# Second feed-forward layer in four parts of 6, 6, 4 and 6 blocks

## The chip, the cores and the metric

The kernel runs on one core of a Trainium2 chip. The metric is the device time of one execution in microseconds (us): 1334.24 us before the change, the median of three runs (1333.27 to 1334.41). TensorE is called PE here, VectorE DVE, ScalarE ACT, GpSimd POOL; SP is the engine that issues the DMAs.

## The reference

One encoder layer on x of shape (1, 1024 tokens, 1024 features), all in float32: two branches (chunked attention and a gated MLP over chunks) and their merge, then a SwiGLU feed-forward network and a final norm. The change touches the last three lines.

```
h = h + merged @ w_out
hn = rmsnorm(h, norm_ffn)
g, up = split(hn @ w_ffn_in)                # 2 x 2816 columns
h = h + (silu(g) * up) @ w_ffn_out          # 2816 -> 1024, the second layer
return rmsnorm(h, norm_final)               # x * rsqrt(mean(x*x) + 1e-6) * gain
```

## The kernel before

Features lie on the 128 partitions and tokens along the free axis; `h` is eight tiles (rows j = 0 to 7) of 128 x 1024. A float32 product is made from three PE passes over operands that are split into a high and a low part (`hi`, `lo`, type fp32r): hi x hi, hi x lo, lo x hi. ACT casts the high part, DVE or POOL subtracts it from the source for the low part.

Both feed-forward layers use a seven-product form (Strassen-Winograd): a 2x2 block product from seven products of sums instead of eight. `moving` names the right operands (b11, t1, t2, b21, t3, b22, t4), and products are called "1" to "7". Each leaves its result in one of three banks of PSUM (`bank_of`): "1" and "2" in c1, "5" and then "3" in c3, "6", "7", "4" in c2. A bank that is written on by the next of its products must first have been added by DVE to `h` or `first_g` (`collect_g`, L1509); that add is called an eviction here.

First layer (the loop at L1439): 22 blocks f of 128 inner features, seven products each of 12 matmuls of 128x512. Its products' evictions, activations and weight sums run on DVE, ACT and POOL beside PE. From product 32 on (L1450) the same loop also makes the weights of the second layer: `weights_g` (L1421) is a generator that for a part c and a row pair r loads two rows of `w_ffn_out`, forms four sums on DVE, casts seven high parts on ACT, subtracts seven low parts on DVE (`products_of`, L1220) and writes them by DMA to `g_dram`. One such group is ten steps; `take(making, 1 + (i % 8 == 0))` takes nine steps every eight products.

Second layer: 18 of the 22 blocks in three parts of six, in the seven-product form. A part has 4 r x 7 = 28 products of nine matmuls of 128x512 (`product_g`, L1502). While part c runs, `operands_g(c + 1)` (L1464) makes the right operands of the next: 21 steps, one per product, with a sum on DVE in 12 of them, a cast on ACT in all, and a low part in all, on DVE or POOL by the table LOW_G (9 and 12 in parts after the first). `prepare_g` (L1492) loads each product's weights from `g_dram` six products ahead. The last four blocks are multiplied plainly (`fo`, `split_act`, and the loop at L1607): for tokens 0 to 511, 512 to 767 and 768 to 1023 in turn, eight rows j of 12 matmuls, each followed by the eviction, ACT's square and scale of the row, and DVE's sum of squares `acc`. `finish(i)` (L1579) reduces the squares on PE (ss), takes the inverse root (a power on POOL), spreads it by PE (bc), and multiplies and stores the rows; it is woven into the next span of tokens.

Order on every engine is that of the code: instructions of one engine run in the order in which the loops issue them.

Of the kernel before, what the change touches and what calls it, by code (L numbers as in the profile page):

```python
# [11 lines left out]
F32 = mybir.dt.float32  # L12
# [4 lines left out]
P = 128  # L17
# [12 lines left out]
PARTS = 3  # L30
LAST = FB - 6 * PARTS
# [17 lines left out]
def encoder_block(ctx: ExitStack, tc: tile.TileContext, xT, w_in, w_v, w_vs, w_att, w_sgu, w_out,  # L49
# [1367 lines left out]
    order_g += [(c, r, p) for c in range(PARTS) for r in range(4) for p in ("1652734" if c else "65734")]  # L1417
    W3 = 3 * P
    g_dram = dram.tile([len(order_g), P, 2 * W3], F32, name="g_dram")

    def weights_g():  # L1421

        for c in range(PARTS):
            for r in range(4):
                rows = [slot(f"fo{c}_{j}") for j in (2 * r, 2 * r + 1)]
                for t, j in zip(rows, (2 * r, 2 * r + 1)):
                    nc.sync.dma_start(t[:, :2 * W3], w_ffn_out[j][:, c * 2 * W3:(c + 1) * 2 * W3])

                def sums():
                    t = slot(f"gs{c}_{r}", (P, 2, HALF))  # L1430
                    return t[:, 0, :W3], t[:, 1, :W3]

                yield from products_of(f"gw{c}_{r}", rows, W3,
                                       lambda p, t: nc.sync.dma_start(g_dram[order_g.index((c, r, p))], t), sums)
# [4 lines left out]
    for i in range(last_pair - 5):  # L1439
# [10 lines left out]
        if i >= MAKE_FROM:  # L1450
            take(making, 1 + (i % 8 == 0))
# [6 lines left out]
    staged, right_g, act = {}, {}, {}  # L1458
# [5 lines left out]
    def operands_g(c):  # L1464

        low = []
        one, two = ([staged.pop(6 * c + 3 * i + k) for k in range(3)] for i in range(2))
        x = {n: [t[:, halves[h]] for t in ts] for n, ts, h in
             (("b11", one, 0), ("b12", one, 1), ("b21", two, 0), ("b22", two, 1))}
        x.update(t1=x["b11"], t2=x["b11"], t3=x["b12"], t4=x["b21"])  # L1470
        sums = dict(t1=("b12", "b11"), t2=("b22", "t1"), t3=("b22", "b12"), t4=("b21", "t2"))
        n = 0
        for name in ("b11", "t1", "t2", "b21", "t3", "b22", "t4") if c else ("b11", "b21", "t1", "t2", "t3", "b22", "t4"):
            right_g[c, name] = []
            for k in range(3):
                src = x[name][k]
                if name in sums:
                    y, z = (x[m][k] for m in sums[name])
# [192 lines left out]
```

## Time and profile before

| what | value |
| --- | --- |
| median of the three timed runs | 1334.24 us |
| profiled execution, its span | 1334.2 us, 1332.5 us |
| PE busy, share of the span | 1308.0 us, 98% |
| DVE busy | 932.4 us, 70% |
| ACT busy | 571.6 us, 43% |
| POOL busy | 422.6 us, 32% |
| mean granted clock of PE | 0.996 of full speed |
| last chain, PE's share | 58% |

The span runs from the first to the last instruction of the profiled execution. Busy shares are averages over the whole program. The chain is followed back from the last instruction to what released each. Matmuls overlap in PE's pipeline, so the mean length of one (about 390 ns) is not what it costs; that is read from a long stretch without a gap, divided by its count.

### The profile page before, as it was taken

The page shows a single profiled execution, that of the slowest core. Times are in us where ns is not written, and L with a number is a line of the kernel's source. Part 1 is how long each engine was busy: PE and PEld are TensorE (multiplying, and loading weights), DVE is VectorE, ACT ScalarE, POOL GpSimd, SP SyncE. Part 2 cuts the span into 40 slices and gives each one's busy share as a digit, 9 for nine tenths or more (in the row PEclk, how much of TensorE's full clock was granted, in tenths as well). Part 3 has the DMA queues.
Part 4 walks back from the last instruction along what each step waited for, and adds up shares of the span by engine and source line. Part 5 has one row for each costly group of instructions (what it writes and reads, how often), then busy time and mean ns, then how long its engine had stood idle before and what let it go on. Part 6 is the DMA issues. An engine that isn't in the chain of part 4 may idle for free.

```text
span 1332.5 us, 17516 instructions
## 1 busy us (share of the span) xinstructions
PE 1308.0 (98%) x6290; PEld 1085.4 (81%) x6290; DVE 932.4 (70%) x1510; ACT 571.6 (43%) x1056; POOL 422.6 (32%) x343
## 2 busy tenths in 40 slices
PE   9999999999999999999999999999999999999997
PEld 7888888878887877888887888887888887888887
DVE  6257877871869778677867487878878857757445
ACT  7345666663434534454443034444444433212144
POOL 2525444324457345530000021221222222424242
PEclk9999999999999999999999999999999999999999
DMA  6001101003041221259873566666667658786723
GB/s 253 28 17 40 29 28 36 26 25 95 17 166 32 63 64 56 64 199 339 325 296 133 193 232 216 228 229 228 217 223 241 232 191 324 265 286 211 239 57 127
DMA packets 77879, 208.79 MB, mean 157 GB/s; under 512 B 8544, under 2 KB 12128, under 8 KB 77792
## 3 DMA queue, kind: packets, MB, share of 16 engines
q1 hardware_dynamic: 77792, 207.67, 45.3%
q8 instruction: 50, 0.82, 0.3%
q14 instruction: 37, 0.30, 0.1%
HBM read 140.01 MB, written 67.63 MB: 156 GB/s over the span
## 4 chain that ended last, share of the span: by engine, by line
PE 58%; DVE 3%; DMA 1%; issue 1%; ACT 0%; POOL 0%; DVEq 0%; ACTq 0%; POOLq 0%
PE c L182 41%; PE wo L1207 7%; PE mc L182 5%; PE last L168 3%; PE mp L182 2%; DMA g<-g_dram 1%; DVE gw L1227 0%; DVE s L1148 0%; DVE mergedlo L781 0%; DVE t3l L173 0%; DVE exact L1411 0%; DVE gs L1239 0%; DVE u L1360 0%; PE bc L276 0%; ACT wm_hi L155 0%
## 5 line engine op out<-in xcount | busy, mean ns | idle before, releaser
L1183 POOL TENSOR_TENSOR w_lo<-s,w_hi 128x512 fp32r<-128x512 f32 x54 | 77.8, 1443 | 324.4 <-ACT w_hi L1177 324.4
L182 PE MATMUL c<-t,g 128*128 128x512 f32 x432 | 103.7, 390 | 0.0
L182 PEld LDWEIGHTS c<-t,g 128*128 128x128 f32 x432 | 80.7, 188 | 18.3 <-DMA g<-g_dram 1.1
L1518 DVE TENSOR_TENSOR h_all<-h_all,c 128x512 f32<-128x512 f32 x72 | 49.0, 686 | 53.6 <-PE c L182 52.6
L1177 ACT CAST w_hi<-s 128x512 fp32r<-128x512 f32 x72 | 44.7, 621 | 93.9 <-DVE s L1148 93.7
L182 PE MATMUL c<-b,g 128*128 128x512 f32 x324 | 78.4, 389 | 0.4 <-DMA g<-g_dram 0.4
L182 PEld LDWEIGHTS c<-b,g 128*128 128x128 f32 x324 | 60.7, 188 | 13.4 <-issue 0.8
L504 ACT ACTIVATE p<-p,low 128x640 f32<-128x640 f32 (+4 forms) x64 | 44.6, 697 | 58.6 <-DVE low L496 58.4
L1482 ACT CAST t<-stage 128x512 fp32r<-128x512 f32 x36 | 22.2, 623 | 73.5 <-DVE stage L1479 68.1
L156 POOL TENSOR_TENSOR wm_lo<-wg,wm_hi 128x512 fp32r<-128x512 f32 x21 | 30.1, 1437 | 64.0 <-ACT wm_hi L155 60.2
L1207 PE MATMUL wo<-mergedhi,wo_hi 128*128 128x512 f32 x128 | 50.0, 391 | 0.0
L1207 PE MATMUL wo<-mergedhi,wo_lo 128*128 128x512 f32 x128 | 49.8, 389 | 0.0
L1207 PE MATMUL wo<-mergedlo,wo_hi 128*128 128x512 f32 x128 | 49.8, 389 | 0.0
L496 DVE CUSTOM_DVE_ANT_0 p<-s,bias 128x640 f32<-128x640 f32 (+4 forms) x64 | 41.7, 651 | 10.9 <-PE s L492 8.9
L260 POOL TENSOR_TENSOR rms_y<-rms_a,minus_half 128x4 f32<-128x4 f32 (+2 forms) x6 | 6.1, 1014 | 135.3 <-DVE rms_a L255 135.3
L1246 ACT CAST gw<-fo 128x384 fp32r<-128x384 f32 x60 | 30.4, 509 | 43.1 <-DMA fo<-in_w_ffn_out 19.2
L173 POOL TENSOR_TENSOR t<-stage,t 128x512 fp32r<-128x512 f32 x18 | 26.8, 1492 | 61.2 <-ACT t L1482 56.9
L522 DVE TENSOR_TENSOR ptl<-t,pth 128x640 fp32r<-128x640 f32 (+4 forms) x64 | 41.7, 651 | 4.5 <-ACT pth L521 4.2
L168 PE MATMUL last<-act_hi,fo 128*128 128x256 f32 (+1 forms) x192 | 43.8, 320 | 0.0
L1227 DVE TENSOR_TENSOR gw<-fo,gw 128x384 fp32r<-128x384 f32 x60 | 42.2, 703 | 0.9 <-ACT gw L1246 0.8
L506 DVE TENSOR_SCALAR p<-p,inv 128x640 f32<-128x640 f32 (+4 forms) x64 | 39.6, 619 | 2.2
L1357 ACT ACTIVATE g<-g 128x512 f32<-128x512 f32 x22 | 13.9, 633 | 62.8 <-DVE g L1356 62.8
(428 smaller groups left out, 4236.9 us busy)
## 6 DMA issues: line engine op xcount, KB each, us to landing
g_dram<-gw SPq DMA_DIRECT2D x84, 384.0 KB, 2.6
g<-g_dram SPq DMA_DIRECT2D x84, 384.0 KB, 3.7
f_dram<-fw SPq DMA_DIRECT2D x28, 512.0 KB, 4.1
act_dram<-u SPq DMA_DIRECT2D x44, 256.0 KB, 2.3
stage<-act_dram SPq DMA_DIRECT2D x22, 512.0 KB, 6.5
fg<-in_w_ffn_in SPq DMA_DIRECT2D x18, 512.0 KB, 5.0
fu<-in_w_ffn_in SPq DMA_DIRECT2D x18, 512.0 KB, 4.4
fo<-in_w_ffn_out SPq DMA_DIRECT2D x24, 384.0 KB, 4.5
```

The costliest lines, as they stand in the source:

```text
L168: nc.tensor.matmul(ps, w, x[:, s], start=k == 0 and i == 0, stop=k == kc - 1 and i == 2)
L182: nc.tensor.matmul(ps, w[:, ws], x, start=first and k == 0 and n == 0, stop=k == last and n == 2, skip_group_check=True)
L496: nc.vector.tensor_tensor_reduce(out=p[:, :w].rearrange("p (a c) -> p a c", a=parts), in0=ps[:, :parts, :c], in1=bias.rearrange("p (a c) - ...
L504: nc.scalar.activation(e["p"], e["p"], AF.Exp, bias=e["low"], scale=-1.0, accum_out=e["tot"])
L506: nc.vector.tensor_scalar(e["p"], e["p"], e["inv"], None, op0=OP.mult)
L522: nc.vector.tensor_tensor(out=lo[:, :w], in0=ps[:, :w], in1=hi[:, :w].bitcast(F32), op=OP.subtract)
L1177: nc.scalar.copy(hi, src)
L1183: nc.gpsimd.tensor_tensor(out=lo, in0=src, in1=hi.bitcast(F32), op=OP.subtract)
L1207: nc.tensor.matmul(banks_w[j, half], w, x, start=k == 0 and n == 0, stop=k == KB - 1 and n == 2, skip_group_check=True)
L1227: nc.vector.tensor_tensor(out=t[:, width:2 * width], in0=src, in1=t[:, :width].bitcast(F32), op=OP.subtract)
L1246: nc.scalar.copy(t[:, :width], src)
L1518: nc.vector.tensor_tensor(out=dst, in0=dst, in1=banks_g[name, r], op=OP.add)
```

## The change

The 22 blocks are taken in four parts of 6, 6, 4 and 6 (`SIZES`), all in the seven-product form; the plain blocks, their weights and their operands go. A product of the part of four has six matmuls instead of nine, and its weights are 128x256 instead of 128x384. `weights_g` has 16 groups instead of 12 and is advanced by three steps every two products. Operands of the last part are made from the fourth product of the part of four on (`OPERANDS_AT`). The last part follows its own order (`LAST_G`): its first 20 products finish the first 512 tokens and all of the other products but "5" and "3", which are done last, for tokens 512 to 767 and then 768 to 1023. Squares, scale and `finish` follow there row by row; the sum of squares of the first of these spans moves to POOL. The last eight weights lie in the general pool of slots.

```diff
-PARTS = 3
-LAST = FB - 6 * PARTS
+SIZES = (6, 6, 4, 6)
+BASES = (0, 6, 12, 16)
+PARTS = len(SIZES)
-H_AT, STAGE_AT = (0, 3, 5, 7), (8, 9, 11, 12, 13, 14)
+H_AT, OPERANDS_AT = (0, 3, 5, 7), (14, 12, 3)
+STAGE_AT = (8, 9, 11, 12, 13, 14, 33, 34, 35, 36, 51, 53, 55, 58, 60, 62)
+LAST_G = "10 11 12 20 13 21 60 22 61 23 70 62 71 40 63 41 72 73 42 43 50 51 30 52 31 53 32 33"
...
-    order_g += [(c, r, p) for c in range(PARTS) for r in range(4) for p in ("1652734" if c else "65734")]
+    order_g += [(c, r, p) for c in range(PARTS - 1) for r in range(4) for p in ("1652734" if c else "65734")]
+    order_g += [(PARTS - 1, int(x[1]), x[0]) for x in LAST_G.split()]
+    widths = [n // 2 * P for n in SIZES]
...
-            take(making, 1 + (i % 8 == 0))
+            take(making, 1 + (i % 2 == 0))
...
-    fo = [block(f"fo{j}", w_ffn_out[j][:, PARTS * 6 * P:], LAST * P, keep=hi_lo_slot,
-                lo_engine=nc.vector if j == 1 else None) for j in range(KB)]
...
-            t = wpool.tile([P, D], F32R, name=f"g{i}", tag=("raw", "raw", "hi", "lo", "hi", "lo")[i % 6])
-            nc.sync.dma_start(t[:, :2 * W3].bitcast(F32), g_dram[i])
+            w = widths[order_g[i][0]]
+            if i < len(order_g) - 8:
+                t = wpool.tile([P, D], F32R, name=f"g{i}", tag=("raw", "raw", "hi", "lo", "hi", "lo")[i % 6])
+            else:
+                t = slot(f"g{i}", dt=F32R)
+            nc.sync.dma_start(t[:, :2 * w].bitcast(F32), g_dram[i][:, :2 * w])
...
-        if p == "4" and c == PARTS - 1:
+        if c < PARTS - 1:
+            return
+        if p == "1":
             for row, half in ((0, 1), (1, 1), (1, 0)):
                 dst = h[2 * r + row][:, halves[half]]
                 nc.gpsimd.tensor_tensor(out=dst, in0=dst, in1=first_g[:, r], op=OP.add)
+        elif half == 0:
+            square_row(2 * r + row, 0)
+    def square_row(j, i):
+        s = slice(*token_parts[i])
+        x = h[j][:, s]
+        if n_squares[i] > 1:
+            (nc.gpsimd if i == 1 else nc.vector).tensor_tensor(out=acc[:, s], in0=acc[:, s], in1=squares[i], op=OP.add)
+        squares[i] = tmp(f"sq3_{i}_{j}")[:, :x.shape[1]] if n_squares[i] else acc[:, s]
+        nc.scalar.activation(squares[i], x, AF.Square)
+        nc.scalar.activation(x, x, AF.Copy, scale=g_fin[:, j:j + 1])
+        n_squares[i] += 1
...
-        prepare_g(i + 6)
+        if i == len(order_g) - 8:
+            break
+        prepare_g(i + 6 + 8 * (i > len(order_g) - 20))
...
+        if c < len(OPERANDS_AT) and n == OPERANDS_AT[c]:
+            coming = operands_g(c + 1)
...
+    end = finish(0)
+    for i, (a, b) in enumerate(token_parts[1:], 1):
+        cols = slice(a - HALF, b - HALF)
+        for n, m in enumerate(range(len(order_g) - 8, len(order_g))):
+            c, r, p = order_g[m]
+            if p == "5":
+                banks_g["c3", r] = dense_ps(f"c3_{i}_{r}")
+            ps = banks_g["c3", r][:, :b - a]
+            multiply(ps, parts_g[m], [[x[:, cols] for x in k] for k in right_g[c, moving[p]]], p == "5")
+            j = 2 * r + (p == "5")
+            dst = h[j][:, a:b]
+            nc.vector.tensor_tensor(out=dst, in0=dst, in1=ps, op=OP.add)
+            square_row(j, i)
+            take(end, {1: 1, 3: 2, 4: 1, 5: 1, 6: 1}.get(n, 0))
         drain(end)
         end = finish(i)
```

Three places show how instructions move. The first is DVE in the first layer's loop while the second layer's weights are made; before, `gs`, `fo` and `gw` are the sums, the loaded rows and the low parts of that work, the other names belong to the first layer.

```order
L1243 TENSOR_TENSOR fo_2_7249<-fo_2_7249 128x384
L1227 TENSOR_TENSOR gw_1_6_7389<-fo_2_7249,gw_1_6_7389 128x384
L1148 TENSOR_TENSOR s_7_7418<-fu_7209 128x512
L173 TENSOR_TENSOR w_lo<-fg_7207,w_hi 128x512
L1227 TENSOR_TENSOR gw_1_3_7414<-fo_2_7249,gw_1_3_7414 128x384
L1227 TENSOR_TENSOR gw_1_4_7438<-fo_3_7250,gw_1_4_7438 128x384
L1148 TENSOR_TENSOR s_7_7446<-s_7_7418,fg_7207 128x512
L1365 TENSOR_TENSOR u_6_7462<-c_6_7348,sg_7273 128x512
L1366 TENSOR_TENSOR u_6_7462<-u_6_7462,sg_7273 128x512
```

The same work after the change (line numbers are two or three higher):

```order
L1242 TENSOR_TENSOR gs_1_7253<-fo_3_7210 128x384
L1230 TENSOR_TENSOR gw_1_2_7283<-fo_2_7209,gw_1_2_7283 128x384
L1244 TENSOR_TENSOR fo_2_7209<-gs_1_7253,fo_2_7209 128x384
L1230 TENSOR_TENSOR gw_1_5_7308<-gs_1_7253,gw_1_5_7308 128x384
L1151 TENSOR_TENSOR s_6_7319<-fg_7081,s_6_7287 128x512
L1246 TENSOR_TENSOR fo_2_7209<-fo_2_7209 128x384
L1230 TENSOR_TENSOR gw_1_6_7313<-fo_2_7209,gw_1_6_7313 128x384
L1151 TENSOR_TENSOR s_6_7341<-fg_7081,fu_7083 128x512
L1354 TENSOR_TENSOR p_6_7357<-c_6_7344,sg_7281 128x512
```

Of nine instructions six instead of four belong to the weights of the second layer.

The second place is DVE while operands of a next part are made: before, those of the third part during the second, whose products have nine matmuls. `c_1_2` is a bank of part 1, r = 2 (counted from 0); rows at L1518 are evictions, L1479 sums, L173 low parts.

```order
L1518 TENSOR_TENSOR h_all<-h_all,c_1_2_10602 128x512
L1479 TENSOR_TENSOR stage_10468<-stage_10512,stage_10468 128x512
L173 TENSOR_TENSOR t_2_2_10647<-stage_10497,t_2_2_10647 128x512
L1518 TENSOR_TENSOR h_all<-h_all,c_1_2_10619 128x512
L1479 TENSOR_TENSOR stage_10482<-stage_10527,stage_10482 128x512
L173 TENSOR_TENSOR t_2_0_10663<-stage_10468,t_2_0_10663 128x512
L1518 TENSOR_TENSOR h_all<-h_all,c_1_2_10602 128x512
L1479 TENSOR_TENSOR stage_10497<-stage_10541,stage_10497 128x512
```

After, those of the last part (`t_3`) during the part of four, whose products have six:

```order
L1527 TENSOR_TENSOR h_all<-h_all,c_2_1_11065 128x512
L1484 TENSOR_TENSOR stage_10888<-stage_10984,stage_10888 128x512
L176 TENSOR_TENSOR t_3_2_11100<-stage_10952,t_3_2_11100 128x512
L1527 TENSOR_TENSOR h_all<-h_all,c_2_1_11052 128x512
L1484 TENSOR_TENSOR stage_10921<-stage_11006,stage_10921 128x512
L1527 TENSOR_TENSOR first_g<-first_g,c_2_2_11131 128x512
L1484 TENSOR_TENSOR stage_10952<-stage_11032,stage_10952 128x512
L1527 TENSOR_TENSOR h_all<-h_all,c_2_2_11145 128x512
```

Between two evictions DVE has about the same instructions as before, and PE two thirds of the matmuls.

The third place is PE in the last spans of tokens. Before, each row j has a bank of its own, twelve matmuls long (the last rows of row 4 and the first of row 5 around the spread):

```order
L168 MATMUL last_4_11470<-act_lo,fo_11273 128x256
L168 MATMUL last_4_11470<-act_hi,fo_11273 128x256
L276 MATMUL bc_0_11488<-ident,rms_0_y 128x128 x4
L168 MATMUL last_5_11497<-act_hi,fo_11296 128x256
L168 MATMUL last_5_11497<-act_lo,fo_11296 128x256
```

After, products "5" and "3" of one r share a bank (`c_1_3` is c3 of the span 1, r = 3):

```order
L185 MATMUL c_1_3_11691<-t_3_0_11074,g_11491 128x256 x3
L185 MATMUL c_1_3_11691<-t_3_1_11087,g_11491 128x256 x3
L185 MATMUL c_1_3_11691<-t_3_2_11100,g_11491 128x256 x3
L185 MATMUL c_1_2_11652<-b_3_0_11233,g_11503 128x256 x3
L185 MATMUL c_1_2_11652<-b_3_1_11246,g_11503 128x256 x3
L185 MATMUL c_1_2_11652<-b_3_2_11259,g_11503 128x256 x3
L185 MATMUL c_1_3_11691<-b_3_0_11233,g_11519 128x256 x3
```

Between "5" of r = 3 and "3" of r = 3, which must find that bank evicted, stands one product of nine matmuls.

## Rows read from the trace of the kernel before

**Rows 1.** Chain of waits, from 930 us: start, length, engine, name, line, count.
```profile
931.95 181.19 PE c L182 x798
1113.15 10.69 DMA g<-g_dram
...
1132.88 141.12 PE c L182 x621
1274.00 26.07 PE last L168 x132
...
1305.16 8.63 PE last L168 x72
...
1322.93 0.38 PE ss L1587 x2
```
**Rows 2.** Windows, PE: stretch, length, busy (count), clock, DMA share, GB/s.
```profile
848.53:862.63 14.10, 13.59 (x60) 1.00 0.52 197
922.73:931.95 9.22, 8.15 (x37) 1.00 0.54 174
1113.15:1132.88 19.73, 19.34 (x81) 1.00 1.03 407
```
**Rows 3.** What PE waited for, 674 to 1333: total, times, longest, us.
```profile
PE c L182 <- ACT sg L1346: 1.1, 1, 1.1
...
PE c L182 <- ACT w_hi L1177: 0.5, 1, 0.5
PE c L182 <- DMA g<-g_dram: 0.4, 1, 0.4
```
**Rows 4.** Windows, busy of PE, PEld, DVE, ACT, POOL; clock, DMA share, GB/s.
```profile
800.00:1080.00 280.00, 278.42 (x1227) 229.81 (x1226) 226.60 (x342) 118.54 (x225) 64.48 (x44) 1.00 0.64 224
...
1240.00:1280.00 40.00, 40.00 (x178) 33.11 (x178) 18.55 (x25) 4.78 (x7) 15.79 (x12) 1.00 0.53 157
```
**Rows 5.** Lines, 800 to 1080, DVE: busy us, mean ns, idle before.
```profile
L1227 DVE TENSOR_TENSOR gw<-fo,gw 128x384 fp32r<-128x384 f32 x55 | 38.4, 698 | 0.9 <-ACT gw L1246 0.8
...
L1148 DVE TENSOR_TENSOR s<-s,fg 128x512 f32<-128x512 f32 x14 | 13.9, 996 | 0.0
...
L1360 DVE TENSOR_TENSOR u<-c,p 128x512 f32<-128x512 f32 x15 | 10.4, 691 | 12.5 <-PE c L182 12.5
...
L1237 DVE TENSOR_TENSOR gs<-fo,fo 128x384 f32<-128x384 f32 x11 | 6.1, 552 | 5.1 <-DMA fo<-in_w_ffn_out 5.1
```
**Rows 6.** Lines, 800 to 1080, POOL.
```profile
L1183 POOL TENSOR_TENSOR w_lo<-s,w_hi 128x512 fp32r<-128x512 f32 x44 | 64.5, 1467 | 217.8 <-ACT w_hi L1177 217.8
```
**Rows 7.** Timeline, 858 to 862: start, length, engine, line, operation.
```profile
859.05 1.35 POOL L1183 TENSOR_TENSOR w_lo<-s,w_hi 128x512 fp32r<-128x512 f32 x1 [2.22 <-ACT w_hi L1177]
859.18 1.64 DVE L1243 TENSOR_TENSOR fo<-fo 128x384 f32<-128x384 f32 x1
...
860.74 0.54 DVE L1227 TENSOR_TENSOR gw<-fo,gw 128x384 fp32r<-128x384 f32 x1
```
**Rows 8.** Lines, 1060 to 1280, second layer.
```profile
L1518 DVE TENSOR_TENSOR h_all<-h_all,c 128x512 f32<-128x512 f32 x72 | 49.0, 686 | 53.6 <-PE c L182 52.6
L173 POOL TENSOR_TENSOR t<-stage,t 128x512 fp32r<-128x512 f32 x18 | 26.8, 1492 | 61.2 <-ACT t L1482 56.9 <-PE c L182 4.4
L1479 DVE TENSOR_TENSOR stage<-stage,stage 128x512 f32<-128x512 f32 x27 | 25.1, 934 | 0.0
...
L173 POOL TENSOR_TENSOR b<-stage,b 128x512 fp32r<-128x512 f32 x13 | 17.2, 1332 | 34.4 <-ACT b L1482 32.2 <-DMA g<-g_dram 2.0 <-POOL t L173 0.2
...
L173 DVE TENSOR_TENSOR t<-stage,t 128x512 fp32r<-128x512 f32 x18 | 14.9, 828 | 0.5 <-ACT t L1482 0.2
```
**Rows 9.** Timeline, DVE, 1146 to 1148.
```profile
1146.08 0.68 DVE L1479 TENSOR_TENSOR stage<-stage,stage 128x512 f32<-128x512 f32 x1
1146.68 0.68 DVE L173 TENSOR_TENSOR t<-stage,t 128x512 fp32r<-128x512 f32 x1
```
**Rows 10.** Timeline of the first finish, 1302 to 1308.
```profile
1302.03 1.02 POOL L260 TENSOR_TENSOR rms_y<-rms_a,minus_half 128x4 f32<-128x4 f32 x1 [10.40 <-DVE rms_a L255]
...
1304.06 0.42 ACT L1618 ACTIVATE sq<-h_all 128x256 f32<-128x256 f32 x1 [2.48 <-DVE h_all L1614]
...
1304.51 0.51 ACT L1619 ACTIVATE h_all<-h_all,vec 128x256 f32<-128x256 f32 x1
...
1306.15 0.57 ACT L1594 COPY rstd<-bc 128x512 f32<-128x512 f32 x1
1306.74 0.69 DVE L1598 TENSOR_TENSOR h_all<-h_all,bc 128x512 f32<-128x512 f32 x1 [1.22 <-ACT rstd L1594]
1306.79 2.75 POOL L1598 TENSOR_TENSOR h_all<-h_all,rstd 128x512 f32<-128x512 f32 x2 [3.74 <-ACT rstd L1594]
```

More of the change, by code (lines that the diff above doesn't have):

```diff
@@ L1425, in weights_g @@
                 rows = [slot(f"fo{c}_{j}") for j in (2 * r, 2 * r + 1)]
+                w = widths[c]
                 for t, j in zip(rows, (2 * r, 2 * r + 1)):
[L1427 removed]
+                    nc.sync.dma_start(t[:, :2 * w], w_ffn_out[j][:, BASES[c] * P:BASES[c] * P + 2 * w])
                 def sums():
                     t = slot(f"gs{c}_{r}", (P, 2, HALF))
[L1431 to L1434 removed]
+                    return t[:, 0, :w], t[:, 1, :w]
+                yield from products_of(f"gw{c}_{r}", rows, w,
+                                       lambda p, t: nc.sync.dma_start(g_dram[order_g.index((c, r, p))][:, :2 * w], t), sums)
     others = iter(())
@@ L1466, in operands_g, with tile_of @@
         low = []
[L1467 to L1470, printed above, removed]
+        n_half = SIZES[c] // 2
+        def tile_of(name, k):
+            row, col = {"t1": (0, 0), "t2": (0, 0), "t3": (0, 1), "t4": (1, 0)}.get(name, None) or [int(m) - 1 for m in name[1:]]
+            return staged[BASES[c] + n_half * row + k][:, halves[col]]
         sums = dict(t1=("b12", "b11"), t2=("b22", "t1"), t3=("b22", "b12"), t4=("b21", "t2"))
         n = 0
-        for name in ("b11", "t1", "t2", "b21", "t3", "b22", "t4") if c else ("b11", "b21", "t1", "t2", "t3", "b22", "t4"):
+        for name in {0: "b11 b21 t1 t2 t3 b22 t4", PARTS - 1: "b11 b21 t1 t2 t3 t4 b22"}.get(
+                c, "b11 t1 t2 b21 t3 b22 t4").split():
             right_g[c, name] = []
-            for k in range(3):
-                src = x[name][k]
+            for k in range(n_half):
+                src = tile_of(name, k)
                 if name in sums:
-                    y, z = (x[m][k] for m in sums[name])
+                    y, z = (tile_of(m, k) for m in sums[name])
                     nc.vector.tensor_tensor(out=src, in0=y, in1=z, op=OP.subtract)
@@ L1604, in finish @@
             yield 1
-    end = iter(())
-    for i, (a, b) in enumerate(token_parts):
-        s = slice(a, b)
-        for j in range(KB):
-            ps = dense_ps(f"last{i}_{j}")[:, :b - a]
-            drain(half_unit(fo[j], act, s, ps))
-            if i == 0 and j + 1 < KB:
-                begin(fo[j + 1])
-            nc.vector.tensor_tensor(out=h[j][:, s], in0=h[j][:, s], in1=ps, op=OP.add)
-            if 1 < j:
-                nc.vector.tensor_tensor(out=acc[:, s], in0=acc[:, s], in1=squares[i], op=OP.add)
-            squares[i] = tmp(f"sq3_{i}_{j}")[:, :b - a] if j else acc[:, s]
-            nc.scalar.activation(squares[i], h[j][:, s], AF.Square)
-            nc.scalar.activation(h[j][:, s], h[j][:, s], AF.Copy, scale=g_fin[:, j:j + 1])
-            if i:
-                take(end, {2: 1, 4: 2, 5: 2, 6: 1}.get(j, 0))
+    end = finish(0)
[12 more added lines that the diff above has]
+            take(end, {1: 1, 3: 2, 4: 1, 5: 1, 6: 1}.get(n, 0))
         drain(end)
```

33 lines of the change are left out of this document (10 added, 23 removed).

## The prediction

> **What bounds the kernel now.** I read the chain of waits first. From 931.95 us to 1313 us it is PE almost alone: 798 matmuls, a wait for second-layer weights, 621 matmuls in a row and then the plain last blocks [rows 1]. So in the stretch that the change rewrites, a matmul removed is time removed, as long as DVE, POOL and the DMAs still keep ahead. Two long runs give PE's price: 141.12 / 621 = 0.2272 us per 128x512 matmul, 8.63 / 72 = 0.1199 us per 128x256 [rows 1]. Then I read what PE loses: while the second layer's weights are made, 0.51 us and 1.07 us in two windows, where length and busy time differ [rows 2], put down to a late copy and a late cast on ACT, 1.1 and 0.5 us [rows 3]. At the start of the second layer it is 0.39 us, for weights, while DMAs move 407 GB/s [rows 2, 3]. Last I read how full DVE is: 226.60 of 280 us, 81%, in the first layer's loop beside 44 POOL instructions, 18.55 of 40 us, 46%, in the third part, where no operands are made [rows 4].
>
> **PE's work.** The plain blocks have 8 x 12 = 96 matmuls of 512 and 2 x 96 = 192 of 256: 96 x 0.2272 + 192 x 0.1199 = 44.83 us. They go. The part of four has 28 x 6 = 168 of 512: 38.17 us. A part of six has 252 of 512, 57.26 us; the new last part has 20 x 9 = 180 of 512 and 2 x 8 x 9 = 144 of 256, 40.90 + 17.27 = 58.16 us, 0.90 more. Net 38.17 + 0.90 - 44.83 = -5.76 us. The reductions and spreads on PE stay as many. Casts and low parts of the four plain blocks go too, but they lie beside PE in that uncrowded stretch, so they give nothing. The twelve POOL adds of `first_g` come at the start of the last part instead of its rows' ends, beside few DVE instructions: nothing. Their cover is the five products, some 10 us, between the first add and the first eviction into such a row ("6" of r = 0); without it that eviction would wait.
>
> **Making the weights in the first layer: +2 us (0 to +5).** A group has 7 low parts and 4 sums on DVE. A 128x512 instruction takes 0.68 us but the next starts after 0.60 [rows 9]; a 128x384 one has 0.552 undisturbed [rows 5], so I estimate a pitch of 0.47, and 0.335 for 128x256 by the same slope. Twelve groups of 11 x 0.47 = 5.2 us become twelve and four of 3.7 us: +15 us of DVE. Steps go from 120 to 160 and from 9 per 8 products to 3 per 2, so both end after some 107 products of 12 x 0.2272 = 2.73 us, 292 us: DVE's share rises by 5 points from 81%. The twelve wide groups fare worse than this average: their steps come a third faster, as the first pair of listings shows. There DVE runs above the 81% that lost 1.6 us in two places [rows 2, 4]. The lower end is no loss beyond that: DVE still idles 12.5 us in front of one group of evictions alone, waiting for PE [rows 5]. The upper end is four times the present loss less itself, 5 us. I take about twice it anew, near the lower, +2. The 28 more writes and reads of 256 KB fall where DMA shares are 0.52 to 0.64 [rows 2, 4]: nothing; a cast that waits for a slot would otherwise add to this term.
>
> **Operands of the last part during the part of four: +3.9 us (+1.8 to +6.8).** A product there lasts 6 x 0.2272 = 1.363 us instead of 2.045. The 21 steps, 12 sums and 9 low parts on DVE and 12 low parts on POOL, come one step per product, so in 29 us, not 43. What must keep up is the eviction: "7" and "4" of one r share a bank with only "3" between. I count DVE's queue from the end of "5" of r = 1 until "7" of r = 3 is evicted: 16 evictions and 20 sums and low parts, 36 x 0.60 = 21.6 us [rows 9], and the last eviction takes 0.69 to its end [rows 8]. PE reaches "4" of r = 3 after 17 products, 23.2 us. Without disturbance this fits with 0.9 us to spare. But seven POOL low parts lie in it, and they delay DVE. At 859.05 POOL starts a low part of 1.35 us, and the DVE instruction of 859.18, normally 0.54, takes 1.64: it ends 0.42 us behind POOL's, 1.10 late [rows 7]. Evictions, which have one source in PSUM, stay at 0.686 and 0.691 us [rows 5, 8]; those with both sources in SBUF average up to 0.996 [rows 5]. The delay of one POOL instruction, three ways: summed over the lines of the first layer's loop, from 55 at 698 ns against 540 down to 11 at 552, it is about 30 us for 44 of them, 0.68 [rows 5, 6]; in the second layer, where 0.25 x 27 + 0.14 x 18 us and smaller groups make 12.2 us for 18 + 13 POOL instructions, 0.39 [rows 8]; in the one instance, 1.10 [rows 7]. So the stall is 21.6 + 0.7 + 7 x 0.39 - 23.2 = 1.8 us, with 0.68 it is 3.9, with 1.10 6.8. I take 0.68, since DVE is as full there as in the first layer's loop, or fuller. Weights and staged activations also come at some 375 GB/s (384 KB per 2.045 us or 256 KB per 1.363, and 512 KB for each of six activations in 18 us), which is below the 407 GB/s at which 0.39 us were lost [rows 2]; I put that at nothing, with 1.5 us as its upper end.
>
> A rule of the Trainium skill bears on this, "SBUF — State Buffer", section "Who interferes with whom": a DVE instruction with two SBUF inputs and a GpSimd instruction that reads SBUF share a pair of ports, the first holds it for its whole instruction, and the other blocks completely. The trace agrees in the instance at 859 us and in the undisturbed evictions [rows 5, 7]; by the rule a full queue loses nearer 1.1 us than 0.39 each time. That case is a rival below, priced from the rows.
>
> **The last two spans: +1.8 us (+0.8 to +3).** Eight rows of a span took PE 96 x 0.1199 = 11.5 us and now take 8.63. ACT still has eight times 0.42 + 0.51 and gaps, 0.95 each, and the copy of 0.57: 8.2 us [rows 10]. POOL has the power of 1.02, two multiplies in 2.75 and now six sums, at some 0.8 each an estimate at a little over half of one 512-wide multiply's 1.38: 8.6 us [rows 10]. Product "3" of r = 3 needs its bank evicted after only one product of 1.08 us, and that eviction stands on DVE behind a multiply that waits for ACT's copy. Walking through the queue I get waits of about 0.95, 0.2 and 0.6 us, and none of the old tail (PE's last reduction starts at 1322.93 [rows 1], and 9.6 us follow to the span's end) is saved: +1.8. The lower end is only the one wait behind the copy, the upper is PE's whole saving of a span, 2.9.
>
> **Sum.** -5.76 + 2 + 3.9 + 1.8 = +1.94 us on the profiled 1334.2 us (span 1332.5 and 1.7 around it; the median is 0.04 higher): 1336.2 us. Differences under 0.2%, 2.7 us, cannot be told from none, so I forecast no change that can be measured, on the slow side.
>
> **Rivals.** *The cover holds.* Banks and DVE's idle time absorb the denser work: no new loss in the first layer, 0.3 us in the part of four, 0.8 at the end, -4.7 us, 1329.6. For it: DVE idles 53 us before evictions in the second layer [rows 8], and PE lost only 1.6 us in the loop at 81%. Against it: in the part of four the spare time is 0.9 us before POOL's delays. *POOL's lock counts in full.* In the part of four, DVE's queue is full, so each of seven POOL low parts costs 1.10 us; 6.8 instead of 3.9, 1339.1, slower, and slower than can be mistaken from a delay of 0.8 us on (4.7, 1337.0). For it the instance [rows 7]; against it the mean of 0.39 in this layer [rows 8]. *Making overruns the first layer.* Wide groups push DVE past PE for stretches of products and PE waits for a bank there, +5 instead of +2: 1339.2, slower. For it the two losses that exist [rows 2]; against it that the average stays at 86%.
>
> **Chances.** Forecast 0.40 (own range 1332.5 to 1339), cover holds 0.30 (1328.5 to 1331.5), lock in full 0.18, making overruns 0.12 (both 1336 to 1342). Faster by over 0.2% means under 1331.6: 0.27 of the second and 0.03 of the first, 0.30. Slower, above 1336.9: 0.17 of the first, 0.15 and 0.09 of the last two, 0.41. Between: 0.29. The range 1329.0 to 1340.5 leaves about 0.1 on either side.
>
> **What would show it.** In the profile after: PE's busy time less by about 6 us; in the part of four, gaps in PE of some 4 us put down to DVE's evictions, in the second half of its 28 products; DVE near 100% there and sums of about 1 us or more; in the first layer's loop a PE loss of 3 to 4 us instead of 1.6; spans of about 9.5 us at the end where PE has 8.6. PE without gaps in the part of four would prove the sum wrong and leave the first rival; waits for `g<-g_dram` there would show that I undervalued the DMAs.

## The result: 1.2% slower, and where the time went

The changed kernel takes 1350.54 us (median of four runs, 1350.31 to 1351.21) against 1333.85 us: ratio 1.0125, interval 1.0113 to 1.0137. The profiled execution took 1350.7 us, its span is 1349.0. PE's granted clock was 1.00, the level of 2.4 GHz, in every window shown here; in the last 52 us of the span it was 0.94 both before and after.

Two rows split the loss. The second layer's first product has nine matmuls among those of the first layer's last block; in the timeline of PE (start, length, engine, line, operation, count) it stands, before:

```profile
1098.00 2.20 PE L182 MATMUL c<-b,g 128*128 128x512 f32 x9
```

and after:

```profile
1115.08 2.20 PE L185 MATMUL c<-b,g 128*128 128x512 f32 x9
```

So 17.1 us are lost ahead of the second layer, where the change only makes more groups of weights at a faster pace. From that row to the end of the span it took 1332.5 - 1098.0 = 234.5 us before and 1349.0 - 1115.1 = 233.9 after: the rewritten layer itself is 0.6 us faster.

What PE waited for after, from 640 to 1350 us (total, times, longest), answers to [rows 3]:

```profile
PE c L185 <- ACT w_hi L1180: 10.1, 6, 2.6
PE c L185 <- DVE h_all L1527: 2.4, 3, 1.5
PE bc L279 <- DVE rms_y L266: 1.9, 2, 1.7
PE c L185 <- ACT sg L1349: 1.8, 3, 1.1
PE c L185 <- DVE g L1357: 1.5, 1, 1.5
...
PE c L185 <- DVE h_all L1632: 1.0, 2, 0.7
```

The 0.5 us for `w_hi`, a cast of the first layer's weights on ACT, became 10.1. Ahead of the second layer the idle time listed grew by 13.3 us in 11 more gaps, and PE's busy time by 3.6 us (from 454.4 to 458.1 from 640 us on, for the same matmuls): a gap costs some 0.3 us more than the idle time shown. Windows of after (busy of PE, PEld, DVE, ACT, POOL) for the first layer's loop, as in [rows 4], and the second half of the part of four:

```profile
800.00:1080.00 280.00, 267.61 (x1166) 217.69 (x1167) 232.95 (x372) 122.57 (x241) 64.42 (x42) 1.00 0.69 243
...
1243.00:1271.00 28.00, 25.16 (x106) 19.18 (x105) 25.97 (x37) 10.26 (x17) 11.03 (x8) 1.00 0.68 201
```

In the loop DVE went only from 81% to 83% while PE lost 10.8 us more than before: the share of DVE alone doesn't explain it. In the part of four DVE is at 93% and PE loses 2.8 us. One group's start, around 1029 us, shows what adds to a full DVE in the loop (timeline of after, of SP, ACT, DVE and PE; in brackets the idle time before and what ended it):

```profile
1019.79 1.89 SPq L1432 DMA_DIRECT2D fo<-in_w_ffn_out  x2
...
1026.12 0.51 ACT L1249 CAST gw<-fo 128x384 fp32r<-128x384 f32 x1 [1.43 <-DMA fo<-in_w_ffn_out]
1027.78 0.51 ACT L1249 CAST gw<-gs 128x384 fp32r<-128x384 f32 x1 [1.15 <-DVE gs L1240]
1028.85 0.62 ACT L1180 CAST w_hi<-s 128x512 fp32r<-128x512 f32 x1 [0.56 <-DVE s L1151]
...
1027.19 0.56 DVE L1240 TENSOR_TENSOR gs<-fo,fo 128x384 f32<-128x384 f32 x1 [3.65 <-DMA fo<-in_w_ffn_out]
1027.66 0.55 DVE L1230 TENSOR_TENSOR gw<-fo,gw 128x384 fp32r<-128x384 f32 x1
1028.13 0.69 DVE L1151 TENSOR_TENSOR s<-fg,fu 128x512 f32<-128x512 f32 x1
1028.73 0.69 DVE L1354 TENSOR_TENSOR p<-c,sg 128x512 f32<-128x512 f32 x1
...
1029.57 0.47 PE L185 MATMUL c<-b22h,w_hi 128*128 128x512 f32 x1 [1.88 <-ACT w_hi L1180]
```

SP issues the loads of the group's two rows at 1019.79 (`fo`, L1432). They land some 7 us later. The group's first sum on DVE (`gs`, L1240) has come to the head of DVE's queue and waits 3.65 us for them; behind it in DVE's order stand the first layer's sum `s` at 1028.13 and the eviction at 1028.73, and behind `s`, on ACT, the cast that PE's product needs. The chain of waits goes the same way (start, length, engine, name, line):

```profile
1018.25 0.57 DVE gw L1230
1018.85 0.88 SPq L1439
1019.79 0.96 SPq L1432
1020.80 6.27 DMA fo<-in_w_ffn_out
1027.25 0.41 issue
1027.66 0.55 DVE gw L1230
1028.22 0.60 DVE s L1151
1028.82 0.60 DVE p L1354
```

Its first two rows show that the load itself is late: on SP it stands behind the write of the last weight of the group before, which waits for that weight's low part on DVE. So a late DVE also sends the next load late. The chain comes to the loads issued at 1002.8, 1039.1 and 1060.5 us in the same way, from DVE through SP.

Over the loop, DVE waited for rows 5.7 us in 4 groups before and 16.1 us in 10 after (waits of DVE, 765 to 1095, before and then after):

```profile
DVE gs L1237 <- DMA fo<-in_w_ffn_out: 5.7, 4, 2.5
...
DVE gs L1240 <- DMA fo<-in_w_ffn_out: 16.1, 10, 3.7
...
DVE gw L1230 <- ACT gw L1249: 6.5, 13, 1.1
```

Two empty steps at a group's start are all that the code puts between a load's issue and its first use, ACT's cast. At nine steps per eight products they are 1.8 products, 4.9 us; at three per two, 1.3 products, 3.6 us, for loads of 4.3 us median [page of after, `fo` of 384 KB]. DVE's first sum comes one step later than the cast. Its lead is read from the timeline, from SP's issue to the time when DVE had come to the sum (the sum's start less its idle time): 6.7 us before, the median of 12 groups, and 4.0 after, of 16. A group of before with a lead of 6.3 us, and no wait:

```profile
1013.67 0.91 SPq L1427 DMA_DIRECT2D fo<-in_w_ffn_out  x2
...
1019.93 0.55 DVE L1237 TENSOR_TENSOR gs<-fo,fo 128x384 f32<-128x384 f32 x1
```

### The profile page after: what moved, and what is told of

It is laid out like the page before. It is cut to its first block, busy times and chain, and to the rows that moved or that the text cites. A ratio compares the mean times of both kernels' runs of the same rounds, so it can differ in the third digit from the quotient of the medians.

```text
span 1349.0 us, 17646 instructions
## 1 busy us (share of the span) xinstructions
PE 1307.3 (97%) x6242; PEld 1078.2 (80%) x6242; DVE 958.3 (71%) x1568; ACT 581.2 (43%) x1086; POOL 430.9 (32%) x351
## 5 line engine op out<-in xcount | busy, mean ns | idle before, releaser
L185 PE MATMUL c<-t,g 128*128 128x512 f32 (+1 forms) x564 | 127.1, 377 | 2.0 <-DVE h_all L1527 1.9
L185 PEld LDWEIGHTS c<-t,g 128*128 128x128 f32 x564 | 101.0, 188 | 23.0 <-DVE h_all L1527 3.0
L185 PE MATMUL c<-b,g 128*128 128x512 f32 (+1 forms) x432 | 97.8, 373 | 1.8 <-DVE h_all L1632 1.0
L1527 DVE TENSOR_TENSOR h_all<-h_all,c 128x512 f32<-128x512 f32 x88 | 59.8, 685 | 52.8 <-PE c L185 51.7
L185 PEld LDWEIGHTS c<-b,g 128*128 128x128 f32 x432 | 76.4, 188 | 17.4 <-DVE h_all L1632 1.4
L1249 ACT CAST gw<-fo 128x384 fp32r<-128x384 f32 (+1 forms) x80 | 38.2, 484 | 59.9 <-DMA fo<-in_w_ffn_out 32.9
L1230 DVE TENSOR_TENSOR gw<-fo,gw 128x384 fp32r<-128x384 f32 (+1 forms) x80 | 52.4, 657 | 4.3 <-ACT gw L1249 4.0
L176 POOL TENSOR_TENSOR t<-stage,t 128x512 fp32r<-128x512 f32 x23 | 33.2, 1449 | 65.1 <-ACT t L1487 48.3
L499 DVE CUSTOM_DVE_ANT_0 p<-s,bias 128x640 f32<-128x640 f32 (+4 forms) x64 | 41.7, 652 | 10.8 <-PE s L495 8.8
L185 PE MATMUL c<-b22h,w_hi 128*128 128x512 f32 x88 | 34.9, 396 | 10.2 <-ACT w_hi L1180 10.1
L518 PE MATMUL t<-ident,p 128*128 128x128 f32 x240 | 37.0, 274 | 1.7 <-DVE ptl L525 1.6
```

The costliest lines, as they stand in the source:

```text
L185: nc.tensor.matmul(ps, w[:, ws], x, start=first and k == 0 and n == 0, stop=k == last and n == 2, skip_group_check=True)
L499: nc.vector.tensor_tensor_reduce(out=p[:, :w].rearrange("p (a c) -> p a c", a=parts), in0=ps[:, :parts, :c], in1=bias.rearrange("p (a c) - ...
L518: nc.tensor.transpose(ps[:, b * P:(b + 1) * P], e["p"][:, b * P:(b + 1) * P], ident)
L1230: nc.vector.tensor_tensor(out=t[:, width:2 * width], in0=src, in1=t[:, :width].bitcast(F32), op=OP.subtract)
L1249: nc.scalar.copy(t[:, :width], src)
L1527: nc.vector.tensor_tensor(out=dst, in0=dst, in1=banks_g[name, r], op=OP.add)
```

## The experiments

Each run has one profile and one time, but the one from product 16 four times and the last three 9 or 10 times. "Start" is where the second layer's first product stands, 1098.0 before and 1115.1 after. The last column holds DVE's waits that are put down to `fo`, from 765 to 1095 us; DVE's waits for ACT's casts of those rows are not in it. How far starts differ by chance is seen from the run without POOL low parts in the part of four: up to the second layer its code is that of after, and its start is 1.7 us later. Smaller differences of single starts say little.

| run | total, us | kernel before beside it | start, us | DVE waits for rows, us |
| --- | --- | --- | --- | --- |
| before, faster pace | 1349.8 | 1334.5 | 1114.5 | 15.7 |
| after, rows five steps earlier | 1355.0 | 1334.5 | 1119.4 | 1.3 |
| after, no sums | 1334.2 | 1334.5 | 1098.4 | none |
| after, begun at product 16 | 1349.6 | 1334.5 | 1113.2 | 14.2 |
| after, sums feed nothing | 1353.8 | 1334.3 | 1117.9 | 18.5 |
| after, sums a step earlier | 1363.3 | 1334.3 | 1127.4 | 39.9 |
| after, no POOL in the loop | 1345.2 | 1334.3 | 1109.7 | 14.3 |
| after, no POOL low parts in the part of four | 1348.9 | 1334.3 | 1116.8 | 15.2 |
| after, one pair of rows for all | 1339.7 | 1333.0 | 1104.2 | 0.6 |
| after, order 1247563 | 1342.9 | 1333.0 | 1107.6 | none |
| after, rows two steps earlier | 1346.7 | 1333.0 | 1111.0 | 11.8 |
| after, both | 1339.3 | 1333.0 | 1102.9 | none |
| before, both | 1331.6 | 1333.1 | 1097.5 | none |
| after, both, from product 20 | 1336.6 | 1333.1 | 1104.1 | none |
| after, both, from product 24 | 1329.6 | 1333.1 | 1097.4 | none |

**The pace alone, on the kernel before.**

```diff
-            take(making, 1 + (i % 8 == 0))
+            take(making, 1 + (i % 2 == 0))
```

> The kernel before with one edit: the weights of the second layer are made at three steps per two products instead of nine per eight; still twelve groups, all 384 wide. The kernel after lost 17.1 us before its second layer began. Theory D (DVE's queue is too full at this pace, because the evictions stand behind the making's sums and low parts): the twelve wide groups are those in whose time all of the after kernel's gaps lay, so nearly the whole loss appears, 1347 to 1351 us. Theory L (the rows of a group are loaded too shortly ahead: two empty steps are now 1.3 products; ACT's first cast waits for them and the first layer's casts stand behind it): 12 of 16 such waits, 1345 to 1350. Rival N (it is the number of groups, slots and DMAs, not the pace): 1334 to 1336.

1349.8 us, 15.4 over the kernel before, the start 16.5 later. The loss is the pace's, not that of four parts, of 16 groups or of the last eight weights' slots. D and L were not told apart.

**Rows five steps earlier.** The group loop holds the loaded rows and loads the next pair after its sixth step.

```diff
...
+            for n, step in enumerate(steps):
+                if n == 5 and k + 1 < len(groups):
+                    load_rows(k + 1)
+                yield step
```

> The kernel after with one edit: the two rows of a group are loaded in the middle of the group before it, some four steps earlier. Pace, instructions on DVE, ACT, POOL and PE stay. L: ACT's and DVE's waits for rows go (32.9 and 19.5 us in the after profile), and with them most of PE's 17 us: 1335 to 1340 us. D: DVE's queue is as full as before, at most 3 us are won: 1347 to 1351.

1355.0 us, 4.5 more than after. This looked like the end of L, and was not: the waits for rows were gone, but two more tiles (slots) of the pool of 36 were held for longer, and waits of casts for writes to `g_dram` took their place. That the slots alone made the loss was not tested. Waits of ACT and DVE in this run:

```profile
ACT gw L1249 <- DMA g_dram<-gw: 29.5, 15, 5.2
ACT gw L1249 <- DVE gw L1230: 20.1, 16, 2.7
...
DVE gw L1230 <- ACT gw L1249: 25.8, 27, 2.8
```

**No sums.** `products_of` casts the loaded rows without the four sums.

```diff
...
-            if p == "7":
+            if not add:
+                s1, s3 = a21, a22
+            elif p == "7":
```

> The kernel after without the four sums of each group of weights (the loaded rows themselves are cast instead, so the second layer's weights are others); loads, casts, low parts and pace stay. DVE has 7 instructions a group instead of 11, 3.3 us instead of 5.2 at 384 wide, less than in the narrow groups that cost nothing. D: most of PE's 17 us goes: 1334 to 1339 us. L: the first cast waits for its rows as before, 1345 to 1350.

1334.2 us, the start at 1098.4: the loss is gone, although ACT still waited 29.8 us for rows, and DVE 31.1 us for ACT's casts, many of them behind those rows:

```profile
ACT gw L1251 <- DMA fo<-in_w_ffn_out: 29.8, 17, 5.7
...
DVE gw L1230 <- ACT gw L1251: 31.1, 28, 3.3
```

This too seemed to speak for D. With four instructions fewer a group, DVE could wait so long and PE lost nothing: late rows without the full work don't make the loss. Whether the full work makes it without late rows, this run can't tell. Since its loop is as fast as before, it shows that the new second layer, with the gaps of its part of four, is worth nearly nothing in the whole.

**Begun at product 16, four steps per three products.**

```diff
-MAKE_FROM = 32
+MAKE_FROM = 16
...
-            take(making, 1 + (i % 2 == 0))
+            take(making, 1 + (i % 3 == 0))
```

> The kernel after with the making begun at product 16 instead of 32, where DVE was half idle, and advanced by four steps per three products instead of three per two: 160 steps in 120 products. D: an eighth less DVE work per product in the crowded loop, the 17 us fall to 5 to 9: 1339 to 1343 us. L: the lead of the loads grows only from 1.3 to 1.5 products, 1345 to 1350. Rival P (the gaps come from groups of 6.7 products falling on the same place in blocks of 7 products): groups of 7.5 products drift faster, so gaps come and go within three blocks, 1340 to 1347.

1349.6 us, ratio 1.0114 to the kernel before (interval 1.0097 to 1.0131): about one us won where D said 8 or more. The waits for rows stayed (DVE 14.2 us), and L's range holds it. The early start had a price of its own, 3.4 us of gaps in PE between 745 and 756 us that after does not have, so the run speaks against D less clearly than its time does.

**Sums that feed nothing.**

```diff
...
+            if apart and p in "7563":
+                x, y = {"7": (a11, a21), "5": (a21, a22), "6": (a11, a22), "3": (a12, a11)}[p]
+                nc.vector.tensor_tensor(out=s3 if p in "73" else s1, in0=x, in1=y, op=OP.subtract)
...
+            if apart:
+                src = {"5": a21, "7": a22}.get(p, src)
```

> The kernel after with the four sums of each group still on DVE, at the same places and widths, but no longer feeding anything: the casts and low parts take the loaded rows (so the second layer's weights are others). DVE has as many instructions as after; what is gone is that ACT's casts wait for DVE's sums. D (amount of work on DVE): 1346 to 1351 us. Theory C (the wait of ACT's in-order queue for sums that stand deep in DVE's queue, with the first layer's casts behind it): 1334 to 1339.

Each cast and low part takes the loaded rows instead. 1353.8 us, above D's range: theory C falls, the casts' waits for sums are not what costs. The first sum still waited for its rows on DVE, 18.5 us.

**Sums a step earlier.**

```diff
...
             finish_lo()
             late_lo.append((p, t, src))
+            if apart:
+                add({"1": "7", "2": "5", "5": "6", "6": "3"}.get(p))
             yield 1
```

> The kernel after with each sum of the weights issued one step earlier, behind the low part of the step before, so that its cast finds it made one step ago. All work and results stay. C: ACT's waits for sums (32 us in the after profile) mostly go, and PE's loss falls from 17 us to under 8: 1334 to 1342. D: 1347 to 1351.

1363.3 us, the worst of all, above both ranges. The first sum now came one step earlier, in the step of the group's first cast. DVE's and ACT's waits:

```profile
DVE gs L1244 <- DMA fo<-in_w_ffn_out: 39.9, 15, 3.8
...
ACT gw L1252 <- DMA fo<-in_w_ffn_out: 33.8, 14, 5.0
```

DVE's wait for rows went from 16.1 to 39.9 us with ACT's unchanged, and the start came 12.4 us later. That made the next theory, W: DVE's queue held by its first sum.

**No POOL in the loop.**

```diff
-                nc.gpsimd.tensor_tensor(out=lo, in0=src, in1=hi.bitcast(F32), op=OP.subtract)
+                nc.scalar.copy(lo, src)
```

> The kernel after with the first layer's low parts that POOL makes replaced by copies on ACT (so those low parts are the sources themselves). DVE's own instructions stay, POOL's lock on them goes, ACT gets some 48 x 0.62 = 30 us more. If DVE is short because POOL holds it up (about 0.7 us for each of POOL's instructions, 30 us in all): 1334 to 1340. If the making's own instructions fill the queue, or ACT's order decides: 1346 to 1352.

The low parts are then copies of their sources. 1345.2 us, 5.3 less than after and between the two ranges. Window of this run, 800 to 1080:

```profile
800.00:1080.00 280.00, 273.96 (x1199) 223.78 (x1198) 208.90 (x379) 147.81 (x292) 0.00 (x0) 1.00 0.71 250
```

DVE is at 75%, less than before the change (81% [rows 4]), and PE still lost 6 us in this stretch. So POOL's hold on DVE makes the loss larger, by about a third, and isn't all of it. The copies gave ACT 25 us more work in this stretch, so the third is not exact.

**No POOL low parts in the part of four.**

```diff
-                low.append((nc.vector if LOW_G[min(c, 1)][n] else nc.gpsimd, lo, src, hi.bitcast(F32)))
+                if c == PARTS - 1 and not LOW_G[1][n]:
+                    nc.scalar.copy(lo, src)
+                else:
+                    low.append((nc.vector if LOW_G[min(c, 1)][n] else nc.gpsimd, lo, src, hi.bitcast(F32)))
...
```

> The kernel after with POOL's twelve low parts of the last part's operands replaced by copies on ACT (so those low parts are the sources themselves); DVE's instructions stay. The part of four shows gaps of 2.8 us in PE put down to DVE's evictions. If POOL's lock makes them, as the prediction's step has it (a queue that fits with 0.9 us to spare without POOL): under 0.5 us of gaps there, the total some 2.5 us less. If DVE's count alone makes them: 2 to 3 us of gaps stay.

These low parts too are copies of their sources. 1348.9 us. Of the gaps in the part of four, 2.8 us after, one of 0.51 was left, and sums on DVE had their undisturbed length (timeline of PE and lines of DVE, 1236 to 1280):

```profile
1262.29 1.66 PE L185 MATMUL c<-t,g 128*128 128x512 f32 x6 [0.51 <-DVE h_all L1531]
```

```profile
L1484 DVE TENSOR_TENSOR stage<-stage,stage 128x512 f32<-128x512 f32 x9 | 6.2, 685 | 0.0
```

From its start (1116.8) to the end this run took 1347.1 - 1116.8 = 230.3 us, 3.6 less than after. POOL's low parts made most of that stall, as forecast.

**One pair of rows for all groups.**

```diff
-                rows = [slot(f"fo{c}_{j}") for j in (2 * r, 2 * r + 1)]
...
+                if not kept:
+                    kept[0] = [slot(f"fo{c}_{j}") for j in (2 * r, 2 * r + 1)]
...
+                rows = kept[0]
...
```

> The kernel after with only the first group's two rows loaded, and used again by all sixteen groups (so the second layer's weights are others). Sums, casts, low parts, writes and pace stay. The runs so far: without sums the loss is gone, but with sums that feed nothing it stays; with POOL's lock taken away DVE is only 72% busy in the worst stretch and PE still loses 8 us; sums issued earlier, which wait 40 us for their rows on DVE instead of 16, cost 13 us more. Theory W (DVE's in-order queue is held by the first sum of a group, which waits for its rows; evictions stand behind it): with no rows to wait for, PE's 17 us fall to under 4, 1334 to 1338 us. D (the number of DVE's instructions): 1347 to 1351.

1339.7 us, the start 10.8 us earlier than after, with all of DVE's instructions in place: most of the loss is the wait for rows. It is 2 us above W's range; D is far off. The edit also takes 30 loads off SP and the DMAs; that this is not what helps is seen from the run with both edits below, which keeps every load and wins as much.

**Order 1, 2, 4, 7, 5, 6, 3.**

```diff
-    def products_of(name, rows, width, put, sums):
+    def products_of(name, rows, width, put, sums, names="1725634"):
...
-        for p in "1725634":
+        for p in names:
...
-                                       lambda p, t: nc.sync.dma_start(g_dram[order_g.index((c, r, p))][:, :2 * w], t), sums)
+                                       lambda p, t: nc.sync.dma_start(g_dram[order_g.index((c, r, p))][:, :2 * w], t), sums, "1247563")
```

> The kernel after with the seven weights of a group made in the order 1, 2, 4, 7, 5, 6, 3 instead of 1, 7, 2, 5, 6, 3, 4: the first three take the loaded rows as they are, so the first sum comes two steps later, some 3.6 us. All work and results stay. W: DVE's wait for rows (16 us) goes nearly, ACT's (33 us, by the first cast) stays: most of the loss won, 1335 to 1342 us. If ACT's wait is what costs: 1347 to 1351. D: 1347 to 1351.

1342.9 us, 7.6 less than after and 0.9 above W's range, with the same work, the same results and ACT's wait for rows at 32.0 us as ever. DVE's sums no longer wait for rows: its first touch of a group is now a low part that needs the first row alone and stands behind ACT's cast. Its waits for casts grew from 6.5 us to

```profile
DVE gw L1230 <- ACT gw L1249: 19.1, 18, 2.4
```

so DVE's waits went down in all from 22.6 to 19.1 us only, the longest from 3.7 to 2.4. So the run shows that it pays to let DVE touch late rows later, and not how the gain divides between shorter waits and their place in the queue.

**Rows two steps earlier.**

The edit is shown against the run with rows five steps earlier. The loads now stand ahead of the group's last low part and its write on SP.

```diff
-                if n == 5 and k + 1 < len(groups):
+                if n == 8 and k + 1 < len(groups):
```

> The kernel after with the next group's rows loaded two steps earlier, ahead of the last low part and its write. With them loaded five steps earlier, the waits for rows became waits for a free slot (29.5 us of ACT's casts behind writes to DRAM) and nothing was won. W: half of the waits for rows go at the price of some waits for slots: 1338 to 1346. D: 1348 to 1352.

1346.7 us, 3.8 less than after, just above W's range.

**Both**, the order and the rows.

```diff
...
-        for p in "1725634":
+        for p in names:
...
+                if n == 8 and k + 1 < len(groups):
+                    load_rows(k + 1)
```

> Both edits, the order 1, 2, 4, 7, 5, 6, 3 and rows two steps earlier. W: 1334 to 1340 us. D: 1348 to 1352.

1339.3 us, as good as having no rows to wait for. Its gaps from 735 us to the second layer, 5.3 us, all lie between 786 and 869. Window of this run:

```profile
880.00:1080.00 200.00, 200.00 (x883) 165.39 (x882) 166.97 (x275) 90.16 (x179) 50.42 (x33) 1.00 0.73 254
```

There PE loses nothing with DVE at 83%, as busy as in the loop after, and wide groups among them.

**Both, on the kernel before at its own pace** (the same edit).

```diff
...
-        for p in "1725634":
+        for p in names:
...
+                if n == 8 and k + 1 < len(groups):
+                    load_rows(k + 1)
...
```

> The kernel before, its pace of nine steps per eight products kept, with the order 1, 2, 4, 7, 5, 6, 3 and the rows loaded two steps earlier. If its two gaps (1.6 us) are waits for rows too: 1332 to 1333 us. If they are DVE's count: 1333.5 to 1335, no change.

1331.6 us (10 runs) against 1333.1, ratio 0.9992 (interval 0.9983 to 1.0001), not told from no change by this. The start came 0.5 us earlier, and of its two gaps one of 0.20 us was left.

**Both, begun earlier and slower, and the last part's operands spread.** From product 20 at 4/3 or from product 24 at 7/5 steps per product, and in the part of four two steps per three products; the edit from 24, beside those of both:

```diff
-MAKE_FROM = 32
+MAKE_FROM = 24
...
-            take(making, 1 + (i % 2 == 0))
+            take(making, 1 + (i % 5 in (0, 2)))
...
-        take(coming, TAKE_G[i] if i < len(TAKE_G) else 1)
+        take(coming, TAKE_G[i] if i < len(TAKE_G) else int(c != 2 or n % 3 != 2))
```

> The kernel after with the order 1, 2, 4, 7, 5, 6, 3, rows two steps earlier, the making begun at product 20 with four steps per three products, and the operands of the last part made at two steps per three products, so that the last four fall into the last part. With the first two edits alone 5 us of gaps were left, all between 787 and 869 us in the first wide groups. W: in the part of four gaps of 2.8 us fall under 1; if the first groups are too dense (DVE's count), the slower pace takes the other 5 us: 1331 to 1334 us; if the early start costs as much again as it did from product 16 (the operands of the first layer are still being made there): 1335 to 1339.

1336.6 us (10 runs), ratio 1.0025 (1.0015 to 1.0035). This is the range for a costly early start: between 754 and 767 PE waited 3.7 us, 2.3 of it for the stored weights of the first blocks.

> As the run from product 20, but begun at product 24 with seven steps per five products, so that a group takes 7.1 products, nearly a block of the first layer. If the gaps come where groups and blocks stand badly to one another (theory P), this pace keeps them so or keeps them apart: 1334 to 1342, or under 1333. If density decides: between the run from 20 and 1337.5, 1333 to 1336.

1329.6 us (9 runs) against 1333.1, ratio 0.9979 (0.9969 to 0.9989): 0.2% faster than the kernel before, nothing left out. Of these 3.5 us, 2 are left against the kernel before with both edits (1331.6). The time lies under the range for density, 1333 to 1336, and in one that was given to the place of the groups, under 1333. All its gaps from 735 to 1290 us (timeline of PE):

```profile
788.97 0.47 PE L185 MATMUL c<-t3h,w_hi 128*128 128x512 f32 x1 [0.45 <-DVE g L1357]
824.79 0.47 PE L185 MATMUL c<-b22h,w_hi 128*128 128x512 f32 x1 [0.20 <-ACT w_hi L1180]
844.28 0.47 PE L185 MATMUL c<-b22h,w_hi 128*128 128x512 f32 x1 [0.21 <-ACT w_hi L1180]
1252.04 1.65 PE L185 MATMUL c<-t,g 128*128 128x512 f32 x6 [0.44 <-DVE h_all L1538]
```

The loop loses 0.9 us, and from the start the kernel takes 1327.6 - 1097.4 = 230.2 us, 4.3 less than before: the rewritten second layer is faster once its own gaps are gone.

## Why the prediction was wrong

**PE's work, -5.76 us: right, as far as the trace tells.** After the start the time fell by 0.6 us with new gaps of 2.8 us in the part of four and 1.2 us in the last spans, seven in all, each of which costs a little more than the idle time shown. With the part of four's gaps taken away but for 0.5 us, 4.2 and 4.3 us appear. PE's busy time, which was to fall by about 6 us, fell by 0.7 in the whole program: behind the start by 4.2, and ahead of it it grew by the 3.6 us that go with the gaps there.

**Part of four, +3.9 us (1.8 to 6.8): right in mechanism, a little large.** The gaps are 0.41, 0.48, 1.54 and 0.38 us, 2.8 in all, put down to DVE's evictions, in the second half of the part. DVE's instructions there (timeline of after, DVE and one of POOL) show POOL's delay, as [rows 7] did; three of six such sums:

```profile
1250.17 0.68 DVE L1527 TENSOR_TENSOR h_all<-h_all,c 128x512 f32<-128x512 f32 x1
...
1250.38 1.28 POOL L176 TENSOR_TENSOR t<-stage,t 128x512 fp32r<-128x512 f32 x1 [3.88 <-ACT t L1487]
...
1250.77 1.45 DVE L1484 TENSOR_TENSOR stage<-stage 128x512 f32<-128x512 f32 x1
...
1254.54 1.50 DVE L1484 TENSOR_TENSOR stage<-stage,stage 128x512 f32<-128x512 f32 x1
...
1257.76 1.18 DVE L1484 TENSOR_TENSOR stage<-stage,stage 128x512 f32<-128x512 f32 x1
```

These three stand beside POOL's low parts and are late by 0.77, 0.82 and 0.50 us against 0.68 undisturbed. All six, one for each of POOL's low parts from 1250 to 1267, are late by 0.48 to 0.83 us, 0.70 in the mean, where 0.68 was taken for seven. The rule of the Trainium skill that was weighed there ("SBUF — State Buffer", "Who interferes with whom") agrees: each of the six ends 0.54 to 0.56 us behind the end of POOL's instruction, so DVE was held to that end, and without POOL's low parts such sums take 0.685 us. What it costs is thus how much of POOL's instruction was left when DVE came to its own; the 1.10 us of the rival was not met in this part. PE waited for no second-layer weights; the rate that the prediction put at 375 GB/s comes to about 367 from its own figures, which changes nothing.

**Last spans, +1.8 us: right in place, a little large.** PE waited 0.75 and 0.20 us for evictions and 0.21 us more for the first spread, 1.2 us. So the rewritten layer was forecast at nearly nothing, and came to -0.6 us.

**Making the weights, +2 us (0 to +5): this step failed; it cost 17.1.** It priced the pace as DVE work, 5 points of its share, and bounded the loss by four times what the two gaps before showed. In its own terms the loop was to lose 3 to 4 us; it lost 12.4 in the window from 800 to 1080. The pace set something else as well, to which the prediction gave no term: how long before its first use a group's rows are loaded. That lead is counted in steps, so a faster pace shortens it in time: to ACT's cast from 4.9 to 3.6 us by the count, and to DVE's first sum from 6.7 to 4.0 in the trace, under the 4.3 to 4.5 us that a load takes. The row for it (`fo`, 384 KB, 4.5 us) was on the page of before and was not put beside the pace. The runs show the parts: with one pair of rows for all 10.8 us go; with sums later and rows earlier 12.2 us; with POOL's low parts of the first layer away 5.4. These overlap. Neither late rows nor DVE's work makes the whole loss alone: without the sums DVE waited 31.1 us and nothing was lost, and with all the work but rows in time 5 to 6 us of 17 stay. That a wait at a group's start costs where DVE cannot catch up before the next eviction is due fits all these runs and was not tested by itself.

The 5 us that stay after both edits went when the making began earlier and slower. Windows of the run with both edits, and then with the making from product 20 and from 24 (busy of PE, PEld, DVE, ACT, POOL):

```profile
786.00:870.00 84.00, 78.70 (x343) 63.60 (x342) 74.92 (x114) 37.01 (x72) 19.74 (x13) 1.00 0.76 269
...
786.00:870.00 84.00, 84.00 (x371) 69.30 (x370) 74.50 (x114) 37.28 (x71) 21.91 (x14) 1.00 0.79 268
...
786.00:870.00 84.00, 83.14 (x365) 67.96 (x364) 74.73 (x114) 38.89 (x74) 16.95 (x12) 1.00 0.73 264
```

DVE is at 89% in all three, and PE loses 5.3, 0.0 and 0.9 us. So DVE's share of this stretch doesn't tell when PE loses; whether the pace or the place of the groups against the blocks decides about these 5 us was not separated.

**The rivals.** That making overruns the first layer (chance 0.12) was the right place at a fraction of the size, and its mechanism, wide groups pushing DVE past PE, was not the main one: with both edits PE loses nothing from 880 to 1080 with DVE at 83%. "The cover holds" was wrong in the part of four and in the loop. "POOL's lock counts in full" named the part of four, where 0.70 us was measured. The time lies above all four cases.

## What to carry to other kernels

When background work is advanced by steps, its pace sets not only the load on the engines but the lead of its loads: put steps times step time beside the landing time of each load, ask what stands ahead of the load on the queue that issues it, and then what stands behind the first instruction that waits. Prefer an order in which the engine with the fullest queue touches late data last. And a run that takes away a wait must be read for the wait that takes its place (here writes that hold slots, and casts behind the rows), before its theory is dropped.

## What the runs showed that was not expected

In the run without sums ACT waited 29.8 us for rows and DVE 31.1 us for casts, and PE lost almost nothing (the start at 1098.4), while 16.1 us of DVE's waits for rows beside the full work went with 17 us lost: the length of the waits doesn't tell their price. Moving two loads five steps earlier cost 4.5 us instead of saving any, with waits for writes in the place of waits for rows. And the changed second layer, which seemed worth 0.6 us, is worth 4.3 us once the operands of its last part are made at two thirds of the pace.
